# First projection of a hybrid encoder layer: output blocks in other tiles, weight loads into the newest free tile, and evacuations written ahead of later operands

## The chip, the core and the metric

The kernel runs on one core of a Trainium2 chip. A core has five engines that run side by side, each with its own queue, which it works off in order: TensorE (PE in the profile; its weight loads are the row PEld), VectorE (DVE), ScalarE (ACT), GpSimd (POOL) and SyncE (SP). POOL and SP do nothing here but issue DMA transfers. Engines wait for each other by semaphores. The metric is the device time of one execution in microseconds; the time of a kernel is the median of its runs.

## The reference, cut to what matters

One layer is computed: a normalised input times one wide projection `w_in`, two kinds of attention on its columns, an output projection, and a gated feed-forward part. The change touches two of the matrix products: most columns of the first projection, and `w_gate` and `w_up`.

```python
def reference(x, attn_norm_w, w_in, ...):
    for l in range(DEPTH):                      # DEPTH = 1
        h = rmsnorm(x, attn_norm_w[l])          # x: 512 rows of 2048
        proj = h @ w_in[l]                      # 2048 x 6176
        aq, ak, av, gq, gk, gv, gr, glr = jnp.split(proj, split_idx, axis=-1)
...
        x = x + mixed
        h = rmsnorm(x, ffn_norm_w[l])
        x = x + (jax.nn.silu(h @ w_gate[l]) * (h @ w_up[l])) @ w_down[l]   # FFN_HIDDEN = 5632
    return rmsnorm(x, final_norm_w)
```

## The kernel before

**Numbers in two parts.** Every fp32 operand of a matrix product is split in two parts of the type that TensorE takes: hi, made by ACT as a cast, and lo, made by DVE as the operand minus hi. A product is hi by hi, hi by lo and lo by hi.

**Units and steps.** Where the change is, weights are worked off in units of 256 columns. A unit's weights are four quadrants (two halves of the rows by two halves of the columns), each a tile of 128 x 1024: 8 blocks of 128 x 128. A block scheme with seven products takes the place of eight: some weight operands are sums of quadrants (`add`, L1538, DVE), and the results are combined again behind the products. Each of the seven steps n = 0 to 6 of a unit is one product: 8 matmuls 128x512 with hi (L1601) and 8 matmuls 128x256 with lo (L1604), all into one bank of PSUM. The class `Front` runs 16 such units for the first projection (columns g of the gate, q and k of both attentions; 112 steps), the class `Feed` 42 units for `w_gate` and `w_up` in turn (294 steps); 406 steps in all. Two units of `Feed` ahead of them are done in another way, which the change leaves as it is but for a call.

**Evacuation.** Behind product n stands its evacuation `evac_(n)`, which reads PSUM:

- n = 0: ACT copies minus X into the bank of Y (L1629), in which product 2 goes on to add. n = 1: ACT copies V to a small tile (L1632).
- n = 2: ACT copies minus Y into the bank of W (L1636), in which product 4 goes on; DVE sets the bank of Z (L1638).
- n = 3, 5, 6: a quarter of the output block, ACT copies one half of the bank (L1623), DVE adds the other (L1624).
- n = 4: DVE adds W to the small tile (L1645) and makes the last quarter (L1647). L1645 reads W, in which product 6 goes on to add: product 6 waits for it.
- behind n = 6, `finish` multiplies the block by a row of factors (in `Front` L1799 or L1801) and POOL writes it to DRAM (L1802).

**The order of the work** is what the code says, step by step. For step i, `fetch` issues loads of quadrants by SP (L1531); `lead(i + 2)` makes the operands of the step after next: `cast` (hi, L1563, ACT), `add` for the step behind that one, and `sub` (lo, L1569, DVE); `evac_late` evacuates product i - 1; `products(i)` issues the matmuls of step i, and `run_urgent` goes on with a `finish`.

**Tiles.** `s4` has 33 tiles of 128 x 1024 (`b` in the profile), `s2` has 36 of 128 x 512 (`a`). `get` takes the tile that has been free longest, `put` appends. A tile's new user waits until its old users are done, the DMA that writes it to DRAM among them. In `Front` the output block is an `s4` tile, as quadrants, sums, hi and lo are; `fetch` keeps up to 8 quadrants loaded as long as more than 3 `s4` tiles are free.

Of the kernel before, what the change touches and what calls it, by code (L numbers as in the profile page):

```python
# [23 lines left out]
P = 128  # L24
# [96 lines left out]
def layer(nc, tc, x, attn_norm_w, w_in, rel_table, gw_f, gb_f, gw_b, gb_b, gla_norm_w, w_out,  # L121
# [7 lines left out]
    with tc.manual_schedule(), \  # L129
# [1381 lines left out]
        class Units:  # L1511

            ORDER = ("B11", "T1", "T2", "B21", "T3", "B22", "T4")
            FREES = {0: "B11", 4: "T3", 5: "B22", 6: "T4"}
            AHEAD, KEEP = 2, 3

            def open(self, first):
# [6 lines left out]
            def fetch(self, most=8):  # L1524
                while self.todo and len(self.quads) < most and len(s4.free) > self.KEEP:
                    u, b = self.todo.popleft()
                    r = self.quads[u, b] = s4.get(F32, [P, NP, P])
                    w, col = self.place(u)
                    k, h = divmod(b, 2)
                    rows = w[:, col + h * P:col + (h + 1) * P].rearrange("(q k p) c -> k p q c", k=2, p=P)  # L1530
                    sp.dma_start(out=r.t, in_=rows[k])  # L1531
# [77 lines left out]
            def evac_late(self):  # L1609
                late, self.late_ = self.late_, []  # L1610
                for i in late:
                    self.evac_(i)

            def evac_(self, i):

# [24 lines left out]
                if n == 3:  # L1640
                    self.outs[u] = s4.get(F32, [P, 2, 512])
                    out("X", 0)
                if n == 4:
                    y = self.parts.pop(u)
                    tt(y.t, y.t, B("W").t, op=OP.add)  # L1645
                    o = self.outs[u].t.rearrange("p f t -> p (f t)")
                    tt(o[:, 768:1024], y.t[:, a], y.t[:, z], op=OP.add)  # L1647
                    put(y)
                if n == 5:
                    out("Z", 1)  # L1650
                if n == 6:
                    out("W", 2)
                    c_ = self.outs.pop(u)
                    urgent.append(self.finish(u, c_, c_.t.rearrange("p f t -> p (f t)")))

        class Feed(Blocks, Units):
# [41 lines left out]
            def evac(self, u, banks):  # L1698
# [21 lines left out]
                yield  # L1720
                yield from self.finish(u, c_, c)
                yield

            def finish(self, u, c_, c):
                w, j = self.units[u]
# [7 lines left out]
                else:  # L1733
                    dve.tensor_tensor(c_.t, c_.t, self.gate.t, op=OP.mult)
                    put(self.gate)
                    pool.dma_start(out=gd[j], in_=c)
                    put(c_)

            def run(self):
# [43 lines left out]
        class Front(Units):  # L1783

            def __init__(self):
                self.units = [(w_in, C_GR + g * 256) for g in range(4)] + [(w_in, C_GQ), (w_in, C_GK)] + \
# [7 lines left out]

            def finish(self, u, c_, c):
                def do():
                    r = rb[1].t[:, None, :].to_broadcast([P, 2, 512])
                    if u in (4, 6):
                        dve.scalar_tensor_tensor(c_.t, c_.t, P ** -0.5, r, op0=OP.mult, op1=OP.mult)  # L1799
                    else:  # L1800
                        dve.tensor_tensor(c_.t, c_.t, r, op=OP.mult)  # L1801
                    pool.dma_start(out=grd[u] if u < 4 else gfd[u - 4] if u < 8 else qkd[u - 8], in_=c)  # L1802
                    put(c_)

# [569 lines left out]
```

## Time and profile before

| what | us |
|---|---|
| median of 3 runs (2162.06 to 2162.73) | 2162.21 |
| the profiled execution, its own time | 2165.34 |
| its span, first to last instruction | 2163.6 |

The profile's instruction times lie within the span; 1.7 us of the profiled execution lie around it. DVE is busy for 1724.6 us of the span, ACT for 1229.1 us, POOL for 172.6 us. `Front` has its products between about 106 and 442 us, `Feed` its 42 units between about 900 and 1720 us; between them are the attentions and the output projection, behind them `w_down`.

A row of a timeline gives the start of a group of instructions, the time that it took, engine, line, operation and tiles; behind it in brackets how long the engine had stood idle and what ended that. Matmuls overlap: a single 128x512 lasts 393 ns, but eight in a row take 2.00 us.

### The profile page before, as it was taken

The numbers are of one execution on the slowest core, as the hardware profiler recorded it, in microseconds if no ns is written. First come the engines' busy times: TensorE is split into PE (matmuls) and PEld (weight loads), VectorE is DVE, ScalarE is ACT, GpSimd is POOL, SyncE is SP. The second block draws the span as 40 slices with busy tenths as digits, with TensorE's granted clock in tenths as the row PEclk, the third lists the DMA queues.
The fourth block names the chain that finished last, engine by engine and source line by source line (L and its number), as shares of the span: only waits on it lengthen the run. The fifth ranks groups of instructions, "written<-read, shape, count | busy, mean of one in ns | idle before, by whom it ended". The sixth has DMA issues, their size and how long they took to land.

```text
span 2163.6 us, 30507 instructions
## 1 busy us (share of the span) xinstructions
PE 2135.8 (99%) x11418; PEld 1835.3 (85%) x11418; DVE 1724.6 (80%) x2345; ACT 1229.1 (57%) x2051; POOL 172.6 (8%) x278
## 2 busy tenths in 40 slices
PE   9999999999999999999999999999999999999998
PEld 7887888888888888988888888888888888888887
DVE  5677787868877657988888888888888878897885
ACT  7444444457786545555545555555555576666762
POOL 0000000112312000000000000000000020232000
PEclk9999999999999999999999999999999999999999
DMA  6543444365754423444434334443344497899572
GB/s 203 172 149 108 136 120 134 105 199 171 201 199 140 134 98 117 137 127 123 116 113 136 116 118 117 127 132 112 114 130 117 173 241 248 200 256 241 194 256 78
DMA packets 340594, 330.47 MB, mean 153 GB/s; under 512 B 15133, under 2 KB 260365, under 8 KB 340446
## 3 DMA queue, kind: packets, MB, share of 16 engines
q1 hardware_dynamic: 313598, 258.07, 39.1%
q0 software_dynamic: 26528, 69.91, 12.5%
q8 instruction: 90, 1.47, 0.3%
q14 instruction: 58, 0.48, 0.1%
q10 hardware_dynamic: 320, 0.53, 0.1%
HBM read 267.55 MB, written 60.92 MB: 152 GB/s over the span
## 4 chain that ended last, share of the span: by engine, by line
PE 83%; issue 13%; DMA 1%; DVE 1%; ACT 1%; POOL 0%; DVEq 0%; SPq 0%; POOLq 0%; ACTq 0%
PE ps L1601 26%; PE ps L1604 14%; PE ps L349 6%; PE ps L350 6%; PE ps L348 6%; PE ps L2057 5%; PE ps L2056 5%; PE ps L2055 5%; PE ps L699 1%; PE ps L2270 1%; PE ps L2272 1%; PE ps L2271 1%; PE ps L643 1%; PE ps L724 1%; PE ps L723 1%
## 5 line engine op out<-in xcount | busy, mean ns | idle before, releaser
L1569 DVE TENSOR_TENSOR b<-b,b 128x1024 fp32r<-128x1024 f32 x406 | 495.2, 1220 | 133.9 <-ACT b L1563 122.0
L1563 ACT CAST b<-b 128x1024 fp32r<-128x1024 f32 x406 | 425.9, 1050 | 200.7 <-DVE b L1569 92.0
L1601 PE MATMUL ps<-a,b 128*128 128x512 f32 x1656 | 427.0, 393 | 16.4 <-DVE a L1645 11.1
L1601 PE MATMUL ps<-b,b 128*128 128x512 f32 x1592 | 421.2, 393 | 0.5 <-ACT ps L1629 0.5
L1601 PEld LDWEIGHTS ps<-a,b 128*128 128x128 f32 x1656 | 304.8, 189 | 81.9 <-issue 13.2
L1601 PEld LDWEIGHTS ps<-b,b 128*128 128x128 f32 x1592 | 280.2, 189 | 43.2 <-ACT ps L1629 0.7
L1538 DVE TENSOR_TENSOR b<-b,b 128x1024 f32<-128x1024 f32 x232 | 282.6, 1218 | 1.3 <-PE ps L350 0.7
L1604 PEld LDWEIGHTS ps<-b,b 128*128 128x128 f32 x1592 | 232.6, 190 | 23.4
L1604 PE MATMUL ps<-a,b 128*128 128x256 f32 x1656 | 242.9, 283 | 0.0
L1604 PE MATMUL ps<-b,b 128*128 128x256 f32 x1592 | 242.8, 282 | 0.0
L1604 PEld LDWEIGHTS ps<-a,b 128*128 128x128 f32 x1656 | 225.2, 192 | 8.5
L1623 ACT COPY b<-ps 128x256 f32<-128x256 f32 x174 | 64.6, 371 | 223.5 <-PE ps L1604 223.5
L2031 DVE TENSOR_TENSOR b<-b,b 128x1024 fp32r<-128x1024 f32 x112 | 136.5, 1220 | 34.8 <-ACT b L2023 34.8
L348 PE MATMUL ps<-b,b 128*128 128x512 f32 x344 | 139.8, 407 | 0.0
L350 PE MATMUL ps<-b,b 128*128 128x512 f32 x344 | 135.1, 393 | 0.0
L349 PE MATMUL ps<-b,b 128*128 128x512 f32 x344 | 134.9, 392 | 0.0
L2023 ACT CAST b<-b 128x1024 fp32r<-128x1024 f32 x112 | 116.6, 1052 | 26.6 <-DVE b L2011 15.3
L220 DVE TENSOR_TENSOR b<-b,b 128x512 fp32r<-128x512 f32 x120 | 79.5, 683 | 26.7 <-ACT b L239 26.5
L1624 DVE TENSOR_TENSOR b<-b,ps 128x256 f32<-128x256 f32 x174 | 72.2, 415 | 27.7 <-ACT b L1623 27.7
L2055 PE MATMUL ps<-b,a 128*128 128x512 f32 x240 | 93.4, 389 | 0.0
L2056 PE MATMUL ps<-b,a 128*128 128x512 f32 x240 | 93.4, 389 | 0.0
L2057 PE MATMUL ps<-b,a 128*128 128x512 f32 x240 | 93.4, 389 | 0.0
(308 smaller groups left out, 3580.6 us busy)
## 6 DMA issues: line engine op xcount, KB each, us to landing
b<-in_w_in_dram SPq DMA_DIRECT2D x94, 512.0 KB, 4.1
b<-in_w_gate_dram SPq DMA_DIRECT2D x88, 512.0 KB, 4.4
b<-in_w_up_dram SPq DMA_DIRECT2D x88, 512.0 KB, 3.8
b<-in_w_down_dram SPq DMA_DIRECT2D x88, 512.0 KB, 6.9
b<-in_w_out_dram SPq DMA_DIRECT2D x32, 512.0 KB, 4.4
md<-a POOLq DMA_DIRECT2D x56, 256.0 KB, 6.8
gd<-b POOLq DMA_DIRECT2D x22, 512.0 KB, 5.3
b<-gd SPq DMA_DIRECT2D x22, 512.0 KB, 5.5
```

What stands on the lines that cost most here:

```text
L348: mm(o, xh.t[:, c], wh.t[:, w], start=first and not on, stop=False, skip_group_check=on)
L349: mm(o, xh.t[:, c], wl.t[:, w], start=False, stop=False, skip_group_check=on)
L350: mm(o, xl.t[:, c], wh.t[:, w], start=False, stop=last, skip_group_check=on)
L1538: tt = lambda o, x_, y_: dve.tensor_tensor(o.t, x_.t, y_.t, op=OP.add)
L1563: act.copy(hi.t, home[key].t)
L1569: dve.tensor_tensor(lo.t, home[key].t, hi.f, op=OP.subtract)
L1601: mm(o.rearrange("p (s t) -> p s t", s=2), hi.t[:, q], self.xs[q][self.ORDER[n]], start=new and q == 0, stop=False, skip_group_check=True)
L1604: mm(o[:, 0:256], lo.t[:, q], self.xs[q][self.ORDER[n]][:, 0], start=False, stop=q == NP - 1, skip_group_check=True)
L2031: dve.tensor_tensor(lo.t, s.t, hi.f, op=OP.subtract)
L2055: mm(o, xh[:, t], wh, start=new and j == 0, stop=False, skip_group_check=True)
L2056: mm(o, xh[:, t], wl, start=False, stop=False, skip_group_check=True)
L2057: mm(o, xl[:, t], wh, start=False, stop=last and j == 1, skip_group_check=True)
```

## The change

In both classes `evac_late`, the evacuation of product i - 1, is now written ahead of `lead(i + 2)`. In `Front` the output block moves from one `s4` tile to two `s2` tiles; the multiplication of `finish` and the write to DRAM become two each, of half the size. `fetch` in `Front` now turns the list of free tiles before it takes one, so a quadrant goes to the tile that was freed last, and in the loop it keeps 6 quadrants loaded and not 8. `home` and `block` say where an output block lives; `Feed` keeps its `s4` tile.

```diff
@@ class Units
+            NEWEST = False
...
             def fetch(self, most=8):
                 while self.todo and len(self.quads) < most and len(s4.free) > self.KEEP:
                     u, b = self.todo.popleft()
+                    if self.NEWEST:
+                        s4.free.rotate(1)
                     r = self.quads[u, b] = s4.get(F32, [P, NP, P])
...
+            def home(self):
+                return s4.get(F32, [P, 2, 512])
+
+            def block(self, u, c):
+                return self.outs[u].t.rearrange("p f t -> p (f t)")[:, c * 256:(c + 1) * 256]
...
                 def out(k, c):
-                    o = self.outs[u].t.rearrange("p f t -> p (f t)")[:, c * 256:(c + 1) * 256]
+                    o = self.block(u, c)
...
                 if n == 3:
-                    self.outs[u] = s4.get(F32, [P, 2, 512])
+                    self.outs[u] = self.home()
...
@@ class Feed, run
                 for i, (u, n) in enumerate(self.steps):
                     self.fetch()
+                    self.evac_late()
                     self.lead(i + self.AHEAD)
-                    self.evac_late()
                     self.products(i)
...
@@ class Front
+            NEWEST = True
...
-            def finish(self, u, c_, c):
+            def home(self):
+                return s2.get(), s2.get()
+
+            def block(self, u, c):
+                f, h = divmod(c, 2)
+                return self.outs[u][f].t[:, h * 256:(h + 1) * 256]
+
+            def finish(self, u, c_):
                 def do():
...
-                    pool.dma_start(out=grd[u] if u < 4 else gfd[u - 4] if u < 8 else qkd[u - 8], in_=c)
-                    put(c_)
+                    d = grd[u] if u < 4 else gfd[u - 4] if u < 8 else qkd[u - 8]
+                    for f, o in enumerate(c_):
+                        if u in (4, 6):
+                            dve.scalar_tensor_tensor(o.t, o.t, P ** -0.5, rb[1].t, op0=OP.mult, op1=OP.mult)
+                        else:
+                            dve.tensor_tensor(o.t, o.t, rb[1].t, op=OP.mult)
+                        pool.dma_start(out=d[:, f * 512:(f + 1) * 512], in_=o.t)
+                    put(*c_)
...
@@ class Front, run
                 for i, (u, n) in enumerate(self.steps):
-                    self.fetch()
+                    self.fetch(6)
+                    self.evac_late()
                     self.lead(i + self.AHEAD)
-                    self.evac_late()
```

How the order of instructions moves is shown at three places. A row is line, operation, output, inputs and size; a name is the tile with its number, then the number of its use; in brackets stand the engines whose semaphores it waits for, DMASW for a DMA that POOL issued, DMAHW for one of SP's. The line numbers of the changed kernel are up to 20 higher: L1563 is L1566, L1569 is L1572, L1629, L1632 and L1636 are L1638, L1641 and L1645, L1623 and L1624 are L1632 and L1633, L1645 and L1647 are L1654 and L1655.

First place: ACT in `Front`, from the evacuation of product 0 of one unit to that of product 3. Before:

```order
L1563 CAST b12_300_2684<-b22_272_2456 128x1024 [waits DMAHW7_49,PE_49]
L1629 ACTIVATE ps6_79_2688<-ps1_78_2663 128x512 [waits PE_49]
L1563 CAST b6_302_2707<-b9_262_2380 128x1024 [waits DMASW1_49,DVE_49]
L1632 COPY a11_69_2712<-ps7_80_2690 128x512 [waits PE_49]
L1563 CAST b9_306_2734<-b29_295_2635 128x1024 [waits DVE_49]
L1636 ACTIVATE ps0_81_2738<-ps6_79_2688 128x512 [waits PE_49]
L1563 CAST b8_308_2758<-b16_257_2332 128x1024 [waits DMAHW4_49]
L1623 COPY b32_311_2764<-ps1_78_2663 128x256 [waits PE_49]
```

The same steps in the changed kernel:

```order
L1638 ACTIVATE ps6_79_2707<-ps1_78_2686 128x512 [waits PE_49]
L1566 CAST b29_289_2709<-b19_273_2575 128x1024 [waits DMAHW7_49,DVE_49]
L1641 COPY a9_87_2730<-ps7_80_2713 128x512 [waits DMASW7_49,PE_49]
L1566 CAST b22_291_2732<-b6_260_2451 128x1024
L1645 ACTIVATE ps0_81_2757<-ps6_79_2707 128x512 [waits PE_49,Activation_49]
L1566 CAST b17_295_2761<-b12_285_2660 128x1024 [waits DVE_49]
L1632 COPY a10_88_2781<-ps1_78_2686 128x256 [waits DMASW0_49,PE_49]
L1566 CAST b16_297_2785<-b18_254_2399 128x1024 [waits DMAHW4_49]
```

Each evacuation has moved ahead of one cast. The cast of step 4 (before: into b6, the tile that held the output block of the unit before) no longer waits for a DMA of POOL's; the waits for POOL's DMAs now stand at the copies into `a` tiles, and are for the blocks of two units before.

Second place: DVE in `Front`, around L1645, from the first addition of the next unit's sums on. Before:

```order
L1538 TENSOR_TENSOR b5_283_2555<-b5_283_2555,b19_284_2557 128x1024 [waits DMAHW2_49,DVE_49]
L1569 TENSOR_TENSOR b6_313_2786<-b19_284_2557,b16_312_2783 128x1024 [waits DMASW1_49,PE_49,Activation_49]
L1645 TENSOR_TENSOR a11_69_2712<-a11_69_2712,ps0_81_2738 128x512 [waits PE_49]
L1647 TENSOR_TENSOR b32_311_2764<-a11_69_2712 128x256 [waits DVE_49]
L1538 TENSOR_TENSOR b9_316_2810<-b5_283_2555,b26_278_2507 128x1024 [waits PE_49]
```

The same instructions in the changed kernel:

```order
L1654 TENSOR_TENSOR a9_87_2730<-a9_87_2730,ps0_81_2757 128x512 [waits DMASW7_49,DVE_49,PE_49]
L1655 TENSOR_TENSOR a11_89_2782<-a9_87_2730 128x256 [waits DVE_49]
L1541 TENSOR_TENSOR b10_280_2629<-b10_280_2629,b30_283_2654 128x1024 [waits DMAHW2_49]
L1572 TENSOR_TENSOR b29_302_2814<-b30_283_2654,b12_301_2811 128x1024 [waits Activation_49]
L1633 TENSOR_TENSOR a10_88_2781<-a10_88_2781,ps4_82_2759 128x256 [waits Activation_49]
```

L1645 (now L1654), for which product 6 waits, has moved ahead of one addition and one subtraction.

Third place: SP, the first loads of quadrants, ahead of `Front`. Before:

```order
L1531 DMA b12_84_935<-in_w_in_dram 128x8x128 [waits DVE_49]
L1531 DMA b5_85_937<-in_w_in_dram 128x8x128 [waits DMASW1_49,PE_49]
L1531 DMA b26_86_939<-in_w_in_dram 128x8x128 [waits DMAHW2_49,DVE_49]
```

In the changed kernel:

```order
L1534 DMA b30_84_935<-in_w_in_dram 128x8x128 [waits DVE_49,PE_49]
L1534 DMA b10_85_937<-in_w_in_dram 128x8x128 [waits DVE_49]
L1534 DMA b8_86_939<-in_w_in_dram 128x8x128 [waits DMAHW2_49]
```

The first load now goes to b30, the tile freed last: the operand of the eighth-last of 16 pieces of the job ahead of `Front` was in it, and the load waits for the matmuls that read it. The loads behind it stand in the same queue.

More of the change, by code (lines that the diff above doesn't have):

```diff
@@ L1645, in evac_ @@
                     tt(y.t, y.t, B("W").t, op=OP.add)
-                    o = self.outs[u].t.rearrange("p f t -> p (f t)")
-                    tt(o[:, 768:1024], y.t[:, a], y.t[:, z], op=OP.add)
+                    tt(self.block(u, 3), y.t[:, a], y.t[:, z], op=OP.add)
                     put(y)
@@ L1653, in evac_ @@
                     c_ = self.outs.pop(u)
-                    urgent.append(self.finish(u, c_, c_.t.rearrange("p f t -> p (f t)")))
+                    urgent.append(self.finish(u, c_))
         class Feed(Blocks, Units):
@@ L1720, in evac @@
                 yield
-                yield from self.finish(u, c_, c)
+                yield from self.finish(u, c_)
                 yield
-            def finish(self, u, c_, c):
+            def finish(self, u, c_):
                 w, j = self.units[u]
@@ L1735, in finish @@
                     put(self.gate)
-                    pool.dma_start(out=gd[j], in_=c)
+                    pool.dma_start(out=gd[j], in_=c_.t.rearrange("p f t -> p (f t)"))
                     put(c_)
```

7 lines of the change are left out of this document (1 added, 6 removed).

## The prediction

> **What bounds the kernel now.** I read the page first, then the windows by stage, then who TensorE (PE) waits for.
>
> ```profile
> PE 2135.8 (99%) x11418; PEld 1835.3 (85%) x11418; DVE 1724.6 (80%) x2345; ACT 1229.1 (57%) x2051; POOL 172.6 (8%) x278
> 106.00:422.00 316.00, 299.62 (x1685) 260.84 (x1684) 250.46 (x272) 145.62 (x197) 9.56 (x18) 0.99 0.43 124
> 900.00:1720.00 820.00, 819.54 (x4693) 720.98 (x4692) 697.12 (x754) 427.00 (x592) 11.17 (x21) 1.00 0.41 122
> PE ps L1601 <- DVE a L1645: 11.1, 12, 1.1
> PE ps L1601 <- ACT ps L1629: 3.5, 1, 3.5
> PE ps L1601 <- ACT ps L1636: 1.7, 2, 1.4
> PE ps L1601 <- ACT ps L1629: 0.5, 1, 0.5
> ```
>
> The kernel is bound by PE: 99% busy, 27.8 us idle in 2163.6. Behind the page's line come two stages, `Front` and `Feed`; columns are stage, its length, then busy time of PE, PEld, DVE, ACT and POOL, granted clock, DMA share and GB/s. PE is idle for 16.4 us in `Front` and for 0.5 us in `Feed`. The last four rows name whom it waited for: three for `Front` (16.3 us in all), one for `Feed`. So the change can win in `Front` only, and in `Feed` it can only lose, half a microsecond aside.
>
> The idle time understates what `Front` loses, since a wait also drains the overlap of the matmuls. The pace of one instruction that comes once in a unit shows the whole:
>
> ```profile
> L1645 DVE TENSOR_TENSOR a<-a,ps x16: 675/678/687, 126.7 to 436.5; 128x512 f32<-128x512 f32 x16
> L1645 DVE TENSOR_TENSOR a<-a,ps x42: 677/679/686, 914.1 to 1714.3; 128x512 f32<-128x512 f32 x42
> ```
>
> Each row has count, shortest, median and longest time in ns, and start of the first and the last. `Front`: 15 intervals in 309.8 us, 20.65 us for a unit. `Feed`: 41 intervals in 800.2 us, 19.52 us, for the same seven products, hardly ever waiting. A unit of `Front` is 1.13 us too long, 17.0 us over 15 intervals.
>
> Why `Front` waits, in one of its units (start, time, engine, line):
>
> ```profile
> 261.20 0.53 POOL L1802 DMA_DIRECT2D gfd<-b  x1 [20.11 <-DVE b L1799]
> 264.18 1.05 ACT L1563 CAST b<-b 128x1024 fp32r<-128x1024 f32 x1 [3.34 <-DMA gfd<-b]
> 265.25 1.23 DVE L1569 TENSOR_TENSOR b<-b,b 128x1024 fp32r<-128x1024 f32 x1 [2.08 <-ACT b L1563]
> 267.60 1.23 DVE L1569 TENSOR_TENSOR b<-b,b 128x1024 fp32r<-128x1024 f32 x1 [1.11 <-ACT b L1563]
> 274.21 0.68 DVE L1645 TENSOR_TENSOR a<-a,ps 128x512 f32<-128x512 f32 x1
> 275.03 2.09 PE L1601 MATMUL ps<-a,b 128*128 128x512 f32 x8 [0.85 <-DVE a L1645]
> ```
>
> POOL writes the last unit's block out; the cast of step 4 goes into that tile and stands 3.34 us until the write has landed. Behind it DVE is idle twice, 3.2 us together. It then works without a gap up to L1645, which ends at 274.89, and product 6 starts at 275.03 after 0.85 us of idle PE. So it is order and one tile, not throughput, that delays PE.
>
> **The change part by part.** *The write leaves the casts' way.* With the block in `s2`, casts in `Front` wait for loads, DVE and ACT only. The first copies into an `a` tile wait for the write of two units before, nearly 20 us old. DVE's work in a unit:
>
> ```profile
> L1569 DVE TENSOR_TENSOR b<-b,b 128x1024 fp32r<-128x1024 f32 x99 | 120.8, 1221 | 56.9 <-ACT b L1563 52.1 <-PE ps L1604 2.6 <-PE ps L1601 1.1
> L1538 DVE TENSOR_TENSOR b<-b,b 128x1024 f32<-128x1024 f32 x56 | 68.2, 1217 | 0.0
> L1624 DVE TENSOR_TENSOR b<-b,ps 128x256 f32<-128x256 f32 x42 | 17.3, 412 | 0.0
> L1801 DVE TENSOR_TENSOR b<-b,a 128x1024 f32<-128x1024 f32 x12 | 14.7, 1225 | 0.4
> L1638 DVE TENSOR_TENSOR ps<-a,ps 128x512 f32<-128x512 f32 x14 | 9.6, 689 | 0.0
> L1647 DVE TENSOR_TENSOR b<-a 128x256 f32<-128x256 f32 x14 | 6.0, 425 | 0.5
> L220 DVE TENSOR_TENSOR b<-b,b 128x512 fp32r<-128x512 f32 x120 | 79.5, 683 | 26.7 <-ACT b L239 26.5
> L1563 ACT CAST b<-b 128x1024 fp32r<-128x1024 f32 x406 | 425.9, 1050 | 200.7 <-DVE b L1569 92.0 <-PE ps L1604 27.8 <-DMA qkd<-b 17.7
> ```
>
> Seven subtractions, four additions, three L1624, one each of L1801, L1638, L1645, L1647: 8.55 + 4.87 + 1.24 + 1.23 + 0.69 + 0.68 + 0.43 = 17.7 us. The multiplication in two halves adds 2 x 0.683 - 1.225 = 0.14 us, if L220, the nearest row of 128x512, is its price. 17.8 us fit in 19.52.
>
> *The new order, step by step.* Time 0 is the start of a unit's product 0, a step is 19.52 / 7 = 2.79 us, and an evacuation starts 0.2 us behind its product's end. Casts take 1.05, copies of 512 columns 0.58, of 256 0.37. Step 3 (at 8.4): L1636 to 9.2, cast 5 to 10.2, L1638 to 9.9, subtraction 5 to 11.5. Step 4 (11.2): L1623 to 11.7, casts 6 and 7 to 13.8; on DVE L1624 to 12.1, an addition to 13.4, subtraction 6 to 14.6. Step 5 (13.9): L1645 to 15.3, L1647, an addition to 16.9, subtraction 7 to 18.1. Step 6 (16.7): L1624 to 18.5, addition to 19.8, subtraction 8 to 21.0. Next unit's step 0 (19.5): L1624, subtraction 9 to 22.6, both halves of the multiplication to 24.0. There DVE waits for the cast of step 3, done at 24.1: nothing is carried over. Product 6 starts at 16.7 and needs L1645 by 15.3: 1.4 us to spare, the least of all needs. So the 17.0 us go, unless an unseen wait takes more than 1.4 us out of a unit. Gain 17.0 us; bounds 0 (DVE's idle only moves) and 17.0.
>
> *The start of `Front`.*
>
> ```profile
> 111.02 0.53 POOL L621 DMA_DIRECT2D vd<-b  x1 [2.21 <-DVE b L618]
> 110.72 1.05 ACT L1563 CAST b<-b 128x1024 fp32r<-128x1024 f32 x1 [0.78 <-DVE b L618]
> 114.18 1.04 ACT L1563 CAST b<-b 128x1024 fp32r<-128x1024 f32 x1 [2.42 <-DMA vd<-b]
> 115.13 0.58 ACT L1629 ACTIVATE ps<-ps 128x512 f32<-128x512 f32 x1
> 115.77 3.30 PE L1601 MATMUL ps<-a,b 128*128 128x512 f32 x8 [3.51 <-ACT ps L1629]
> 120.23 0.62 PE L1587 MATMUL ps<-b,b 128*128 128x512 f32 x2
> 116.00:121.00 5.00, 5.00 (x20) 4.19 (x20) 3.89 (x4) 2.54 (x4) 0.00 (x0) 0.66 0.38 105
> ```
>
> Product 2 waits for L1629, which stands behind cast 3 on ACT, which waits for the write of v to land. With L1629 ahead it starts when cast 2 is done, at 111.8, and ends at 112.4; product 2 follows and ends by 115.2. Cast 3 still ends at 115.2, and L1587, which opens the next banks, follows at about 115.4 and not at 120.23. Gain 4.8 us: 3.5 of wait and the slow clock behind it (granted 0.66 over 5 us; eight matmuls took 3.30 instead of 2.00 us). Bounds 3.3 (the wait but for 0.2, with the slow clock kept) and 5.2.
>
> How much of the slow clock goes if only part of the wait does, no row shows. The Trainium skill, "TensorE: Matmul & The Clock Gate", in its part 1 on the clock gate, says that the clock is halved after an idle window of about 3.4 us, by windows that run free. The row agrees (3.51 us idle, then 0.66). By that rule a wait cut to 2 us would keep the whole clock, 1.7 us won; shared out by length, 0.7 us.
>
> *Loads.* The first quadrant now waits for matmuls that end about 7 x 12 matmuls of 0.2265 us, 19.2 us, ahead of 106.3: at 87.1 and not at 71.6.
>
> ```profile
> 71.56 23.04 SPq L1531 DMA_DIRECT2D b<-in_w_in_dram  x9
> 90.19 2.48 DVE L1538 TENSOR_TENSOR b<-b,b 128x1024 f32<-128x1024 f32 x2 [0.73 <-PE ps L350]
> 106.08 0.39 PE L350 MATMUL ps<-b,b 128*128 128x512 f32 x1
> b<-in_w_in_dram SPq DMA_DIRECT2D x13, 512.0 KB, 6.9
> b<-in_w_in_dram SPq DMA_DIRECT2D x50, 512.0 KB, 4.1
> ```
>
> Landing takes 4.1 us (median in `Front`) to 6.9 (here, where several are under way). So the third load, issued at about 88, lands by 92 to 95, the first casts and sums are done by 94 to 97, and behind them on DVE the last but one weight piece of the job ahead (0.68 us) by 98. PE wants it at 106.3 - 24 x 0.2265 = 100.9. Cost 0, 2.9 us to spare; were landing 3 us longer still, a microsecond or so. Inside `Front` a load is issued at least 14.7 us ahead of its first use (that of quadrant 3: behind product 2, at 8.4, for the cast of step 3 of the next unit, at 19.5 + 3.6); less 4.1, 10.6 us to spare.
>
> ```profile
> 425.46 3.62 POOL L577 DMA_DIRECT2D a<-qkd  x7
> qkd<-b POOLq DMA_DIRECT2D x6, 512.0 KB, 2.9
> 443.36 1.67 ACT L601 ACTIVATE a<-a 128x512 fp32r<-128x512 f32 x3
> ```
>
> Behind `Front` POOL loads q and k back, into `a` tiles that now have just been written out from: the first load waits for the second last unit's write to land, about 2.9 us behind its issue, so it starts some 3 us later than at 425.5. ACT reads them at 443.4; eight issues of 0.53 and one landing are done by 436. Cost 0.
>
> *`Feed`.* The same table holds, with one whole multiplication (1.22 us) in place of the halves and, in every second unit, 1.15 us of ACT for a gate, behind cast 3, where ACT has time. Gain 0 to 0.5 us; I take 0.5.
>
> **Sum** for the profiled execution: 2165.3 - 17.0 - 4.8 - 0.5 = 2143.0 us. The median of the runs lies 3.1 us below that execution, so 2139.9, rounded 2140.
>
> **The rivals.** *DVE's idle time only moves.* Casts now stand behind evacuations, which wait for PE; if hand-overs cost more than the 1.4 us to spare, a shorter wait stays in each unit. For it: DVE is filled to 91%. Against it: `Feed` runs at the same load without waiting. With 0.4 to 1.0 us left of 1.13, 6 to 15 us less gain: 2146 to 2155. The Trainium skill, "VectorE: DVE Perf Modes", in its section on the TRN2 errata, speaks against halves: each instruction from SBUF pays a fixed part, about 150 cycles at 0.96 GHz as measured there, so 0.16 us more in a unit. The rows say 0.14; by either the halves fit, and the sum stays.
>
> *The cause is another.* If the waits came from DVE's order alone, or the new tiles wait like the old ones, the time stays at 2158 to 2165. Against it speaks the row of 264.18.
>
> *Loads come too late (slower).* A quadrant that takes the newest tile can only be loaded when the product that read it is done, and a waiting load blocks SP's queue. That decides from 14.7 us between issue and landing; then each unit waits for the excess. At 18 us it is 3.3 us in 15 units, 50 us against 22 won: 2190. Against it: 4.1 us, with DMA at 43% in `Front`.
>
> **How the numbers follow.** A change under 0.2% (4.3 us) can't be told from none here. The forecast, 2136 to 2145, gets 0.68; idle time that only moves, 2145 to 2157, 0.16; another cause, no change, 0.07; slower, by late loads above all, 0.09. The range reaches from 2136 to 2155 and leaves out about 0.2. Faster 0.84, same 0.07, slower 0.09.
>
> **What would show it.** In the changed profile's `Front`: no wait of a cast for a DMA that POOL issued, save at the start; PE's waits for the evacuation of W gone; a pace of 19.5 us between those evacuations; no granted clock of 0.66 at 116; `Feed` still at 19.52. Wrong would be: casts waiting for `in_w_in`, PE waiting for subtractions in either class, or a stage outside `Front` that changes by over 2 us, since all tiles behind `Front` get other numbers.

## The result, and the profile after

| kernel | median, us | range, us | runs |
|---|---|---|---|
| before | 2162.14 | 2160.68 to 2162.73 | 4 |
| changed | 2141.86 | 2141.47 to 2143.01 | 4 |

The changed kernel takes 0.9908 of the time before, 95% interval 0.9891 to 0.9925: 20.3 us less by the medians. The profiled executions stand at 2165.34 and 2141.47, 23.9 us apart. Line numbers below are those of the changed kernel; the experiments have them too, but for `finish`: its multiplication and its write are L1817 (or L1819) and L1820 in the changed kernel, L1807 (or L1809) and L1810 in e1, e10, e11 and e12.

First the page's line on busy time, and the windows of both stages (length, busy time of PE, PEld, DVE, ACT and POOL, granted clock, DMA share, GB/s); the third window is the one at the start of `Front` in which the clock was 0.66 before.

```profile
PE 2128.3 (99%) x11418; PEld 1831.6 (86%) x11418; DVE 1732.0 (81%) x2361; ACT 1224.1 (57%) x2051; POOL 181.4 (8%) x294
104.00:420.00 316.00, 315.94 (x1806) 277.51 (x1805) 267.34 (x306) 154.84 (x215) 22.94 (x43) 1.00 0.49 138
880.00:1700.00 820.00, 820.00 (x4693) 721.38 (x4692) 703.42 (x761) 423.69 (x595) 11.17 (x21) 1.00 0.41 123
116.00:121.00 5.00, 5.00 (x31) 4.37 (x30) 5.00 (x7) 2.98 (x4) 0.00 (x0) 1.00 0.05 10
```

PE's idle time in `Front` went from 16.4 us to 0.1, in `Feed` from 0.5 to 0.0, and the slow clock is gone. The length of a stage is read from the first and the last start of its products, by line and operand. These are the rows of `Front` that hold its first and its last, of the kernel before (two) and after (two):

```profile
L1601 PE MATMUL ps<-b,b x416: 389/389/398, 106.3 to 437.9; 128*128 128x512 f32 x139
L1604 PE MATMUL ps<-a,b x480: 274/283/415, 111.1 to 441.7; 128*128 128x256 f32 x160
L1604 PE MATMUL ps<-b,b x416: 389/389/398, 104.4 to 414.5; 128*128 128x512 f32 x139
L1607 PE MATMUL ps<-a,b x480: 277/283/283, 109.2 to 418.4; 128*128 128x256 f32 x160
```

With `Feed` read in the same way, the whole difference of the spans falls into place (us):

| stretch | before | after | difference |
|---|---|---|---|
| ahead of `Front` | 106.3 | 104.4 | -1.9 |
| `Front`, first product to last | 335.4 | 314.0 | -21.4 |
| from there to `Feed` | 454.9 | 455.2 | +0.3 |
| `Feed`, first product to last | 822.9 | 822.0 | -0.9 |
| behind it | 444.1 | 444.1 | 0.0 |

The first row has nothing of the change in it. The two executions already differ at the first matmuls: one of 128x512 takes 0.77 us in the kernel before and 0.47 in the changed one, and where the third group of L457 comes, at 12.60 and at 10.70 us, the whole 1.9 us are there (start and time, before first in each pair).

```profile
9.04 0.77 PE L348 MATMUL ps<-b,b 128*128 128x512 f32 x1
7.85 0.47 PE L348 MATMUL ps<-b,b 128*128 128x512 f32 x1
...
12.60 0.60 PE L457 MATMUL ps<-idn,b 128*128 128x128 f32 x4
10.70 0.60 PE L457 MATMUL ps<-idn,b 128*128 128x128 f32 x4
```

In the twelve profiles of the experiments this stretch took 104.2 to 105.9 us, whatever the kernel. So 1.9 of the 23.9 us are start-up.

The pace, by the evacuation of W (count, shortest, median and longest time in ns, first and last start), for `Front` and `Feed`:

```profile
L1654 DVE TENSOR_TENSOR a<-a,ps x16: 678/680/686, 120.9 to 413.1; 128x512 f32<-128x512 f32 x16
L1654 DVE TENSOR_TENSOR a<-a,ps x42: 678/680/687, 888.7 to 1690.3; 128x512 f32<-128x512 f32 x42
```

292.2 / 15 = 19.48 us in `Front`, 801.6 / 41 = 19.55 in `Feed`; single intervals in the middle of either stage are 19.5 to 19.6 us. One unit of `Front` in the timeline (start, time, engine, line), to be held against the unit of before:

```profile
245.19 1.29 DVE L1817 SCALAR_TENSOR_TENSOR a<-a,a 128x512 f32<-128x512 f32 x2
246.17 1.14 POOL L1820 DMA_DIRECT2D gfd<-a  x2 [18.41 <-DVE a L1817]
248.28 0.59 ACT L1641 COPY a<-ps 128x512 f32<-128x512 f32 x1 [1.26 <-PE ps L1607]
248.76 1.06 ACT L1566 CAST b<-b 128x1024 fp32r<-128x1024 f32 x1
251.13 0.58 ACT L1645 ACTIVATE ps<-ps 128x512 f32<-128x512 f32 x1 [1.31 <-PE ps L1607]
256.88 0.68 DVE L1654 TENSOR_TENSOR a<-a,ps 128x512 f32<-128x512 f32 x1
259.25 2.00 PE L1604 MATMUL ps<-a,b 128*128 128x512 f32 x8
```

The cast of step 4 (248.76) follows the evacuation of step 1 without a wait. L1654 ends at 257.56, and product 6 starts at 259.25 without a wait: 1.69 us to spare.

### The profile page after: what moved, and what is told of

It is laid out like the page before. It is cut to its first block, busy times and chain, and to the rows that moved or that the text cites. A ratio compares the mean times of both kernels' runs of the same rounds, so it can differ in the third digit from the quotient of the medians.

```text
span 2139.7 us, 30612 instructions
## 1 busy us (share of the span) xinstructions
PE 2128.3 (99%) x11418; PEld 1831.6 (86%) x11418; DVE 1732.0 (81%) x2361; ACT 1224.1 (57%) x2051; POOL 181.4 (8%) x294
## 3 DMA queue, kind: packets, MB, share of 16 engines
q0 software_dynamic: 26784, 69.91, 12.7%
q8 instruction: 90, 1.47, 0.3%
## 4 chain that ended last, share of the span: by engine, by line
PE 95%; DMA 1%; issue 1%; ACT 1%; DVE 1%; POOL 0%; SPq 0%; DVEq 0%; POOLq 0%; ACTq 0%
PE ps L1604 35%; PE ps L1607 18%; PE ps L350 6%; PE ps L349 6%; PE ps L348 6%; PE ps L2074 5%; PE ps L2075 5%; PE ps L2073 5%; PE ps L699 1%; PE ps L2290 1%; PE ps L2289 1%; PE ps L2288 1%; PE ps L643 1%; PE ps L1702 1%; PE ps L1701 1%
## 5 line engine op out<-in xcount | busy, mean ns | idle before, releaser
L1572 DVE TENSOR_TENSOR b<-b,b 128x1024 fp32r<-128x1024 f32 x406 | 496.2, 1222 | 99.8 <-ACT b L1566 98.5
L1566 ACT CAST b<-b 128x1024 fp32r<-128x1024 f32 x406 | 421.2, 1052 | 21.1 <-DMA b<-in_w_in_dram 14.9
L1604 PE MATMUL ps<-a,b 128*128 128x512 f32 x1656 | 424.5, 392 | 0.1
L1541 DVE TENSOR_TENSOR b<-b,b 128x1024 f32<-128x1024 f32 x232 | 282.8, 1219 | 12.6 <-DMA b<-in_w_in_dram 12.5
L1632 ACT COPY b<-ps 128x256 f32<-128x256 f32 x126 | 46.9, 373 | 250.8 <-PE ps L1607 228.8
L348 PE MATMUL ps<-a,b 128*128 128x512 f32 x216 | 86.7, 401 | 0.0
```

Of the source, the lines that this page charges most:

```text
L348: mm(o, xh.t[:, c], wh.t[:, w], start=first and not on, stop=False, skip_group_check=on)
L1541: tt = lambda o, x_, y_: dve.tensor_tensor(o.t, x_.t, y_.t, op=OP.add)
L1566: act.copy(hi.t, home[key].t)
L1572: dve.tensor_tensor(lo.t, home[key].t, hi.f, op=OP.subtract)
L1604: mm(o.rearrange("p (s t) -> p s t", s=2), hi.t[:, q], self.xs[q][self.ORDER[n]], start=new and q == 0, stop=False, skip_group_check=True)
```

## The experiments

Each kernel is told by its difference from the kernel before, or from another one. "Front's length" is read as above.

**Each part of the change by itself.** Four kernels; e3 takes two parts at once, the newest tile and the six quadrants:

```diff
e1: Front.run, nothing else
-                    self.lead(i + self.AHEAD)
                     self.evac_late()
+                    self.lead(i + self.AHEAD)
e2: home(), block(), finish() of Front as in the change; order, fetch() and Feed as before
e3: Front
+            NEWEST = True
-                    self.fetch()
+                    self.fetch(6)
e4: Feed.run, nothing else: evac_late() ahead of lead()
```

> Only the order in Front is changed (evacuations ahead of a later step's operands); blocks stay in s4, quadrants take the oldest tile, eight are fetched ahead, Feed keeps its old order. Here the cast of step 4 still takes the tile of the unit before. Theory (a race between one write and one cast): in the kernel before, with a unit's product 0 at time 0, the write lands at 6.7 and the cast could start at 3.6, so it waits 3.1 us. In the new order the multiplication ends at about 4.5, the write lands at about 7.5, and the cast, now behind the evacuation of step 1, could start at 6.4: it waits about 1.1 us, and since no evacuation stands behind it, product 6 does not wait. Front from its first to its last product 314 us (kernel before 335.4, changed kernel 314.0), median 2142 us. Rival A (the tile is the cause, the order mends the start alone): casts wait 2 to 3 us in each unit, pace 20.65 us, Front 331 us, median 2157. Rival B (the order does nothing in a unit nor at the start): 2162.

> Only the blocks of Front move to s2 tiles, multiplied and written out in halves; order, quadrants and Feed as before. Theory: no cast waits for a write out of a block; in the old order the evacuation of W then ends at about 15.9 us of a unit and product 6 needs it at 16.7, so the pace falls to 19.55 us by this alone. At the start the evacuation of step 0 still stands behind the cast that waits for the write of v, so 4.8 us stay. Front 318 to 319 us, median 2147. Rival B (order is the cause in the units): pace stays at 20.65, Front 335, 2162. Rival C (both are needed, each mends a part): pace 19.9 to 20.4, Front 324 to 331, 2152 to 2158.

> Only the quadrants of Front take the tile that came free last, with six fetched ahead in place of eight; blocks stay in s4, order and Feed as before. By the allocation the tile of the written block now goes to the cast of step 5 and not of step 4. Theory (a race): the cast of step 5 could start at about 6.4 us of a unit, the write lands at 5.6 to 6.7, so the wait is 0 to 0.3 us, and the pace falls to 19.55 us although a block's tile is still used. The start keeps its 4.8 us. Front 318 to 319 us, median 2147. Rival A (the shared tile is the cause wherever it goes): pace 20 to 20.65, Front 326 to 335, 2154 to 2162. Rival B (order is the cause): Front 335, 2162. If loads were too late, casts or sums would wait for in_w_in and the time would rise above 2165.

> Only Feed's order is changed (evacuations ahead of later operands); Front is the kernel before. Theory: Feed's products hardly ever waited, so nothing is won but the one wait at its start: Feed from its first to its last product 822.0 to 822.9 us (kernel before 822.9), pace 19.55 us, Front 335.4, median 2161 to 2162.5. Rival: the new order has a price or a gain of its own in Feed of 0.05 us in each of 40 units or more, 2 us or more either way.

| run | median, us | ratio, interval | Front's length, us | Feed's, us |
|---|---|---|---|---|
| e1, order of `Front` | 2180.11 | 1.0070 (1.0057 to 1.0084) | 352.3 | 822.9 |
| e2, blocks in `s2` | 2146.88 | 0.9924 (0.9910 to 0.9937) | 320.1 | 822.9 |
| e3, quadrants newest, six | 2146.98 | 0.9925 (0.9913 to 0.9938) | 319.7 | 822.9 |
| e4, order of `Feed` | 2162.52 | 0.9998 (0.9990 to 1.0007) | 335.4 | 822.0 |

e2 and e3 came out within about 1 us of the theory's figures: either brings `Front` to a pace of 19.55 us, and the start is what stays. e3 is the telling one. It still writes from an `s4` tile that a cast of the next unit takes, only the cast of step 5 and not of step 4, one step of 2.79 us later, and the wait is nearly gone (two casts of step 5 wait, 0.3 and 0.5 us, behind the two writes that took 4.0 and 4.2 us to land and not 2.9). So sharing a tile costs nothing by itself; being first in a race against the write does. e4 changed `Feed` by 0.9 us and the median by nothing that can be told.

e1 was a plain miss: 2142 expected, 2180 measured, 17 us slower than before by the very order that the changed kernel has. One of its units, with its product 0, the write, the cast that takes the tile, and who waits:

```profile
260.13 2.00 PE L1604 MATMUL ps<-b,b 128*128 128x512 f32 x8
266.21 0.53 POOL L1810 DMA_DIRECT2D gfd<-b  x1 [20.41 <-DVE b L1807]
271.95 1.04 ACT L1566 CAST b<-b 128x1024 fp32r<-128x1024 f32 x1 [5.45 <-DMA gfd<-b]
272.90 0.58 ACT L1645 ACTIVATE ps<-ps 128x512 f32<-128x512 f32 x1
273.03 1.23 DVE L1572 TENSOR_TENSOR b<-b,b 128x1024 fp32r<-128x1024 f32 x1 [4.84 <-ACT b L1566]
273.54 1.65 PE L1604 MATMUL ps<-a,b 128*128 128x512 f32 x6 [2.08 <-ACT ps L1645]
```

The write is issued at 266.21 and lands at 271.95. The cast waits 5.45 us, and behind it on ACT stands L1645, the evacuation of step 2, for which PE waits 2.08 us; the expectation had overlooked that one ("no evacuation stands behind it"). Two things make the write late. Product 0 of this unit starts at 260.13, so the write goes out 6.1 us into the unit. In the kernel before it was 3.9, from product 0 at 257.26 to the write at 261.20:

```profile
257.26 2.00 PE L1601 MATMUL ps<-b,b 128*128 128x512 f32 x8
```

And the write takes 5.7 us to land, not 3.0. The groups of transfers show that for the writes of blocks between 120 and 400 us (before) or 410 us (e1; KB each, median us from issue to landing), three rows of before and three of e1:

```profile
qkd<-b POOLq DMA_DIRECT2D x6, 512.0 KB, 2.9
grd<-b POOLq DMA_DIRECT2D x4, 512.0 KB, 3.2
gfd<-b POOLq DMA_DIRECT2D x4, 512.0 KB, 2.9
...
qkd<-b POOLq DMA_DIRECT2D x5, 512.0 KB, 5.6
grd<-b POOLq DMA_DIRECT2D x4, 512.0 KB, 5.5
gfd<-b POOLq DMA_DIRECT2D x4, 512.0 KB, 5.6
```

SP's queue tells why. Loads around that write, and around one in e1 that landed sooner (its write went out at 177.18 and landed at 181.19), and around the write of 261.20 of the kernel before:

```profile
265.91 2.73 SPq L1534 DMA_DIRECT2D b<-in_w_in_dram  x2
...
177.65 1.95 SPq L1534 DMA_DIRECT2D b<-in_w_in_dram  x2
...
263.04 1.00 SPq L1531 DMA_DIRECT2D b<-in_w_in_dram  x2
```

A load that starts 0.30 us ahead of the write: 5.7 us to land. 0.47 us behind it: 4.0. 1.84 us behind it: 3.0. Of the 13 writes of e1 that a cast waited for, the three with the load 0.4 to 0.5 us behind took 4.0 us and the ten with the load ahead 5.5 to 7.6. The Trainium skill, "DMA: Bandwidth & Descriptors", section "Issuing engines are not separate DMA queues", says that transfers issued by SP and by POOL run on the same 16 DMA engines and interleave. The rows agree, and give the price here.

The waits of e1 also cost clock. One wait of PE in it, and the window behind (granted clock third from the end):

```profile
161.82 2.74 PE L1604 MATMUL ps<-a,b 128*128 128x512 f32 x7 [1.93 <-ACT ps L1645]
162.00:167.00 5.00, 5.00 (x20) 4.22 (x21) 4.50 (x6) 2.36 (x3) 0.00 (x0) 0.66 0.00 0
```

Behind waits of 3.92, 2.00 and 2.67 us the windows 230 to 235, 319 to 324 and 408 to 413 us stand at 0.66 too; behind two others of 2.08 and 2.13 us the clock stays at 1.00. Over 106 to 420 us e1 was granted 0.98, an estimated 6 us of its length.

**Which pairs do it.** Two more kernels: e5 is e1 with the blocks of e2; e6 is e1 with one number changed.

```diff
e6 against e1: Front.run
-                    self.fetch()
+                    self.fetch(6)
```

> Front's order and Front's blocks in s2; quadrants take the oldest tile, eight are fetched ahead, Feed keeps its old order. After the first four runs the theory reads: the order alone was slower (2180) because the write out of the block is then issued later in a unit (6.2 us behind the start of its product 0), beside a load, lands 5.5 us later and not 2.9, and the cast of step 4 waits for it with the evacuation of step 2 behind it on ACT. With no block's tile among the casts' tiles the order costs nothing in a unit and takes away the wait at the start. Front 314 to 314.5 us (blocks alone 320.1), median 2141 to 2142, whatever the quadrants do. Rival D (the new order has a price in a unit that only the quadrants' new tiles and the shorter fetch hide, by loads that come at other times): pace above 19.6 us, Front 317 or more, median 2145 or more.

> The kernel of e1 (Front's order alone, blocks in s4, quadrants in the oldest tile) with one number changed: six quadrants fetched ahead in place of eight. By the allocation a written block's tile then goes to the cast of step 2 of the unit but one after, about 35 us behind its write, and no longer to the cast of step 4 of the next. Theory (the slow landing is harmless where no cast needs that tile soon): no cast waits for a write, pace 19.55 us, Front 314 to 315, median 2141 to 2143: 38 us below e1 by one number. Rival D (the order itself costs time in a unit as long as blocks are whole s4 tiles): pace 20.9 to 22.5 as in e1 or between, Front 330 to 352, median 2158 to 2180. If six quadrants in the oldest tiles came too late, casts would wait for in_w_in and the time would lie between.

e5: 2142.31 us, Front 314.4; e6: 2142.43 us, Front 314.0. Both are at the theory's figures, and as fast as the whole change (ratios to before 0.9904 and 0.9902, the change 0.9908). One thing in e6's expectation was read wrongly: the first to take a written tile there is not a cast but a load of the next unit, and SP waits for the write with it. That is seen in who SP waited for in e6 (us in all, times, longest):

```profile
SPq L1534 <- DMA qkd<-b: 79.5, 6, 14.1
SPq L1534 <- DMA grd<-b: 54.1, 4, 14.2
```

SP stands up to 14 us, nobody waits for it, and no load can then start beside the write, which lands 2.9 us (median) after its issue.

**One number alone, and seven in place of six.**

```diff
e9 against the kernel before, e10 against e1: Front.run
-                    self.fetch()
+                    self.fetch(6)      e9
+                    self.fetch(7)      e10
```

> The kernel before with one number changed: Front fetches six quadrants ahead in place of eight (old order, whole blocks in s4, oldest tile, Feed as before). By the allocation the tile of a written block then goes to the cast of step 2 of the unit but one after. Theory (a race between write and next cast in that tile; who takes the tile decides): pace 19.55 us, the start stays (5 to 6 us), Front 319 to 320.5, median 2146.5 to 2147.5, as with the blocks alone and the quadrants alone. Rival G (what helped in those two runs was the new home itself, of blocks or quadrants, such as other loads): Front near 335, median 2160 to 2163.

> The kernel of e1 (Front's order alone) with seven quadrants fetched ahead in place of eight: the written block's tile goes to the cast of step 5 of the unit but one after. Theory: only the cast of step 4 of the very next unit was too early for the write; Front 314 to 315, median 2141 to 2143. Rival (six ahead helped because fewer loads collide with the write, and seven collide like eight): casts still wait, Front 325 to 352, median 2153 to 2180.

e9: 2146.60 us (0.9922, 0.9908 to 0.9935), Front 319.8, as expected: one number gives 16 of the 20 us. As in e6 the first to take the written tile is a load, with which SP waits up to 12.5 us, and not the cast that the expectation names. e3 is this kernel with the newest tile added, and no faster (2146.98, 319.7): what the newest tile does by itself no run shows. e10: 2169.08 us (1.0027, 1.0016 to 1.0037), Front 342.1: slower than before, another miss, at the time of the rival. The tile's next taker had again been looked for among the casts alone. It is the subtraction of step 4 of the very next unit, on DVE:

```profile
260.46 0.53 POOL L1810 DMA_DIRECT2D gfd<-b  x1 [20.93 <-DVE b L1807]
266.55 1.23 DVE L1572 TENSOR_TENSOR b<-b,b 128x1024 fp32r<-128x1024 f32 x1 [4.12 <-DMA gfd<-b]
```

Two loads start 1.27 and 0.32 us ahead of this write, and it lands after 6.1 us.

**Collision, or order?** In e1 and e10 the write is both late and slow. e11 and e12 take the collision away and leave the tile and the order:

```diff
e11 against e1, e12 against e10: Front.finish, behind pool.dma_start(...)
+                    sp.dma_start(out=warm[0:1, 0:16], in_=d[0:1, 0:16])
```

SP waits with this small read for the write to land, so no later load can start beside it.

> The kernel of e1 (Front's order alone, 2180) with one transfer added per unit: right behind each write of a block SP reads 64 bytes of it back, so SP's queue stands until the write has landed and no load of a quadrant can start beside it. The cast of step 4 still takes the written tile. In e1 the loads start 0.3 us ahead of and 2.05 us behind the write, and it lands 5.6 us after its issue. Theory (the collision is the cause of e1's loss, and its lateness feeds itself): the write lands 3.0 us after its issue and is issued some 4.2 us into a unit, so it lands at 7.2; the cast wants to start at 6.4 and waits 0.8 us, the evacuation of step 2 behind it, due at 8.6, is not late. Front 314 to 317, median 2142 to 2145, 35 us or more below e1. Rival H (the order itself makes the write so late, 6.2 us into a unit, whatever it lands in): the write lands at 9.2, the cast waits 2.5 us or more, Front 325 to 345, median 2153 to 2173. Rival I (held loads come too late): casts or sums wait for in_w_in, time above 2150.

> The kernel of e10 (Front's order, seven quadrants ahead, 2169) with the same transfer added. What I told of e10's tiles was incomplete: the first to take a written block's tile there is the subtraction of step 4 of the next unit, on DVE, not a cast two units on, and two loads start 1.27 and 0.32 us ahead of the write, which lands after 6.1 to 6.6 us. Theory (collision): the write lands 3.0 us after its issue, at about 7.2 us of a unit; that subtraction starts at 7.4 in the undisturbed order. Front 314 to 316, median 2142 to 2144. Rival H: the write stays at 5.5 us or later in a unit and DVE waits 1.5 us or more for it, Front 325 to 340, median 2153 to 2168.

| run | median, us | Front's length, us | without the read | stretch from `Front` to `Feed` |
|---|---|---|---|---|
| e11 | 2161.39 | 320.8 | 352.3 (e1) | 466.2 |
| e12 | 2153.99 | 314.2 | 342.1 (e10) | 467.7 |

The medians miss both figures, since the read does harm behind `Front`: behind a late last write it holds SP, and the attention waits for its loads. In e12 that stretch is 12.7 us longer than in e10 (467.7 against 455.0), by waits of PE of 8.4 us and a slow clock behind them (granted 0.50 to 0.61 in the three windows from 450 to 465 us). From who PE waited for behind `Front` in e12 (us in all, times, longest):

```profile
PE ps L723 <- DMA b<-vd: 8.4, 4, 3.8
```

Front's own length answers the question. In e12 it falls by 27.9 us, to that of the changed kernel, as the collision theory had it. In e11 it falls by 31.5 us, and 6.8 us stay above 314.0:

```profile
246.64 2.00 PE L1604 MATMUL ps<-b,b 128*128 128x512 f32 x8
252.74 0.53 POOL L1810 DMA_DIRECT2D gfd<-b  x1 [19.38 <-DVE b L1807]
255.70 1.05 ACT L1566 CAST b<-b 128x1024 fp32r<-128x1024 f32 x1 [2.69 <-DMA gfd<-b]
```

The write now lands 2.96 us after its issue, but it is still issued 6.1 us into the unit (product 0 starts at 246.64) and the cast waits 2.69 us, not 0.8. That part of rival H holds for e11: DVE idles behind the cast, the multiplication comes late, and so does the next write. In e12, where a subtraction takes the tile and waits 0.7 us as a rule, the write goes out 4.6 us into the unit. No cast or sum of either run waits for `in_w_in` inside `Front`, so rival I did not show. Of the 31.5 us that the read wins in e11 some 6 are the clock that e1's waits cost; e11 was granted 1.00 over the same stretch. So most of e1's loss is the collision with what follows from it, and a smaller part the order as long as the cast of step 4 takes the tile.

**The spare.** Extra work for DVE, in the changed kernel, on the way that the prediction calls the tightest:

```diff
e7 (two), e8 (four) against the changed kernel: evac_, n == 4
                     y = self.parts.pop(u)
+                    if isinstance(self, Front):
+                        for _ in range(2):
+                            tt(y.t, y.t, y.t, op=OP.max)
                     tt(y.t, y.t, B("W").t, op=OP.add)
```

> The changed kernel with two more DVE instructions of 128x512 in each unit of Front, right ahead of the evacuation of W that product 6 needs (each takes the larger of a tile and itself, so nothing changes in it). In the trace of the changed kernel that evacuation ends at 257.56 and product 6 starts at 259.23: 1.67 us to spare; the prediction had 1.4. Two more take 1.25 to 1.36 us. Theory (spare as worked out): PE waits 0 to 0.1 us in a unit, Front 314 to 315.5, median 2141 to 2143. Rival E (the spare is used up elsewhere, for instance by the subtractions that come later on DVE): 0.5 to 1.3 us in a unit, median 2150 to 2162.

> As the run before, with four more instructions in place of two: 2.5 to 2.7 us against 1.67 to spare. Theory: product 6 waits 0.8 to 1.1 us in each of 16 units, Front 327 to 332, median 2155 to 2160. If the spare were larger than the table says (rival F, the other instructions of DVE move up into gaps), the time would stay under 2147; if DVE as a whole were the limit (17.8 + 2.7 - 19.5 = 1.0 us in a unit) the sum would be the same, but the subtractions would be waited for too.

e7: 2142.77 us, Front 315.8 (1.0 us of it one wait of PE at the start), intervals of 19.59 to 19.62 us in the middle of `Front`. e8: 2166.91 us, Front 338.7, intervals of 21.07; the changed kernel has 19.55. The extra instructions (L1656) and the evacuation behind them (now L1657), two rows of e7, then three of e8:

```profile
258.59 1.41 DVE L1656 TENSOR_TENSOR a<-a 128x512 f32<-128x512 f32 x2
260.11 0.69 DVE L1657 TENSOR_TENSOR a<-a,ps 128x512 f32<-128x512 f32 x1
...
268.73 2.87 DVE L1656 TENSOR_TENSOR a<-a 128x512 f32<-128x512 f32 x4
271.70 0.69 DVE L1657 TENSOR_TENSOR a<-a,ps 128x512 f32<-128x512 f32 x1
272.53 2.09 PE L1604 MATMUL ps<-a,b 128*128 128x512 f32 x8 [1.27 <-DVE a L1657]
```

Two of them put L1657 off by 1.52 us and lengthen a unit by 0.05; four put it off by 2.97 and lengthen it by 1.51. Either way the spare is 1.47 or 1.46 us. e8 lies above its figure because the expectation counted 0.63 to 0.68 us for an instruction and set 1.67 us of spare against it; a chain in which each needs the one before takes 0.74 to 0.76 us apiece, and some 0.2 us of the 1.67 go for the hand-over to PE (0.14 of it from the end of L1657, 272.39, to the matmul at 272.53). PE waits 16 times for L1657, 20.9 us in all, and for no subtraction, and DVE is busy for 251.5 of the 272.5 us from 150.5 to 423, so the limit is this path and not DVE as a whole.

## Why the prediction was right

The forecast, 2139.9 us, lies 2.0 us below the measured median, inside its likeliest case. Stage by stage 22.3 us were forecast (17.0, 4.8 and 0.5) and 22.0 measured (21.4 and 0.9 won, 0.3 lost between the stages). The mechanism is the one forecast; that the sum comes so close is in part luck, since its terms err in both directions. Point by point:

- **PE waits in `Front` for a cast behind a write: right.** The waits are gone, and e2 and e9 remove them in two ways that share nothing but that they keep the written tile from the cast of step 4 (e3 has the number of e9 in it and is no third way). The pace fell to `Feed`'s, as predicted.
- **17.0 us for the units and 4.8 for the start, 21.8: 21.4 measured in `Front`.** The split was off. The order's part can be read from two pairs that differ in it alone: Front's length falls by 5.7 us from e2 to e5 and by 5.8 from e9 to e6. That is above the 4.8 worked out and above its bound of 5.2. PE waited at the start of e2 as long as before, but the slow clock lay otherwise. The wait and two windows of e2 (granted clock third from the end), then the first of these windows in the kernel before, where only the second was slow:

```profile
PE ps L1604 <- ACT ps L1638: 3.5, 1, 3.5
111.00:116.00 5.00, 2.24 (x5) 1.82 (x6) 3.01 (x4) 2.97 (x4) 0.00 (x0) 0.68 0.47 133
116.00:121.00 5.00, 5.00 (x20) 4.29 (x19) 2.65 (x4) 2.33 (x3) 0.00 (x0) 0.64 0.38 107
...
111.00:116.00 5.00, 1.49 (x11) 1.25 (x10) 1.97 (x2) 2.58 (x4) 0.53 (x1) 1.00 0.78 246
```

  e4, whose `Front` is the code of before, has both windows slow as well (0.73 and 0.59). So that one wait costs more or less by where the slow stretch falls, and the bound was too narrow. Up to its first evacuation of W e2 took 21.5 us and the kernel before 20.4. The units' part is 15.3 to 15.7 us by the lengths of e2, e3 and e9, which pay the dearer start; with that 1.1 us put back, 16.4 by e2 against 17.0. The Trainium skill, "TensorE: Matmul & The Clock Gate", part 1, says that the clock is set by windows that run free of the kernel; the differing slow stretches behind equal waits of 3.5 us agree with it. The prediction's estimate that a wait cut to 2 us would keep the whole clock did not hold in e1, where waits of 1.93 and 2.00 us, well under the idle window of about 3.4 us that it goes by, were followed by 0.66: the measurement decides. No term of the sum rests on it.
- **`Feed`, 0 to 0.5 us: 0.9.** 822.9 us with the old order and 822.0 with the new, in each of ten profiles of the one and four of the other. The wait of 0.5 us is gone; the other 0.4 us were not counted.
- **Loads, cost 0: right.** Ahead of `Front` ACT and DVE wait 14.9 and 12.5 us for the first quadrants (in the groups of the changed kernel, behind the busy time and the mean), and PE waits for none of it. The 14.9 us are one wait, at 93.6; inside `Front` no cast waits for `in_w_in`, as predicted. (7 x 12 x 0.2265 is 19.0 and not 19.2, without effect.)

```profile
L1566 ACT CAST b<-b 128x1024 fp32r<-128x1024 f32 x406 | 421.2, 1052 | 21.1 <-DMA b<-in_w_in_dram 14.9
L1541 DVE TENSOR_TENSOR b<-b,b 128x1024 f32<-128x1024 f32 x232 | 282.8, 1219 | 12.6 <-DMA b<-in_w_in_dram 12.5
```

- **The multiplication in halves, +0.14 us of DVE, hidden: right, and smaller.** Two halves take 1.29 us and the whole 1.22, so 0.07. By the figure of the Trainium skill, "VectorE: DVE Perf Modes", in its section on the TRN2 errata, the estimate was 0.16; the measurement is lower.
- **1.4 us to spare: right, with an offset.** 1.46 to 1.47 us by e7 and e8. Counted as the prediction counts, from the end of L1645 to product 6, it is 1.69; the hand-over to PE, which has no term there, takes the rest.
- **The order and the homes as two terms that add up: only half right.** The prediction gave the order the start and the homes the units, each with its own gain. Alone, the order loses 17 us; beside either of the two changes tried that take the written tile out of the next operands' way it gains 4.2 to 4.6 us over that change by the medians (e6 against e9, e5 against e2).
- **The level: the step that was off by 2 us.** The sum was made against the profiled execution, 2143.0, and 3.1 us were taken off because that execution lay so far above its median. The changed kernel's profiled execution came out 1.5 us below that sum: 1.9 us less at start-up and 0.4 less in `Feed`, 0.4 more in `Front` and 0.3 more behind it. But it lies 0.4 us below its own median, so the 3.1 were not a constant to be taken off: by the comparison of stages 1.9 of them lie in the first 13 us of one execution. Where the other 1.2 are from stays open.

Of the rivals, "DVE's idle time only moves" did not come about in the changed kernel; e1 and e11, where the cast waits behind the evacuations instead of ahead of them, come close to it. "The cause is another" is out with the 20.3 us and the waits that went. The rival by which the time hangs on late loads did not show; loads did harm where no rival of the prediction looked for it, by slowing a write. No kernel of these is faster than the changed one: e5 and e6 equal it, with less changed. Neither has the newest tile, so no run shows a gain from that part.

## What to carry to other kernels

Where an operand waits for a tile that is still being written out, ask first who gets that tile next and when: another count of tiles held ahead and another pool each removed the same wait, a later taker (with the count changed too) all but removed it, and a plan of the tiles must follow every taker, loads and subtractions too, not only the one that waited. Test an order of instructions together with the tiles it runs on, since alone it can lose what it gains beside them. Before a level is forecast, split the profiled execution's distance from its median by stages; start-up differences don't carry over.

## What the runs showed of the hardware

- A 512 KB write issued by POOL landed in 2.9 to 3.0 us as a rule where no load could start beside it (27 of the 32 writes of e11 and e12; one took 3.2 and four 3.9 to 4.5, the cause open). In e1 it took 4.0 us with a load of the same size started 0.47 us behind it (three of three) and 5.5 to 5.8 us with one started 0.3 us ahead (eight of ten; the others 6.3 and 7.6); another load started 2.05 us behind in both cases. In e10 it took 6.1 to 6.6 us (medians) with two started 1.27 and 0.32 us ahead.
- On DVE 128x512 instructions that each need the result of the one before cost 0.74 to 0.76 us apiece (e7, e8), where the duration of one is 0.69.
- Behind a wait of PE of 3.5 us the slow clock lay in one window of 5 us in the kernel before and in two in e2 and e4. In e1 waits of 1.93 to 3.92 us were followed by a window at 0.66 four times, and waits of 2.08 and 2.13 us were not.
